# The tokens' low part in two products of 128 columns, once in each up stage

## The chip, the cores and the metric

The kernel runs on one core of one Trainium2 chip. The metric is the device time of one execution in microseconds; every comparison is between executions on the same chip. The profile shows one execution, with every instruction of the engines: PE is TensorE's matmuls, PEld its weight loads, DVE VectorE, ACT ScalarE, POOL GpSimd, SP the engine that issues the DMAs.

## What is computed

Two layers of an encoder trunk on 256 tokens with a model width of 2048, all in float32:

```python
h = rms_norm(x, g_pre_mix)
proj = h @ w_in                                  # 2048 x 4624
att = window_attention(...); mem = mlstm_mixer(...)
x = x + rms_norm(concat(att, mem) @ w_out, g_post_mix)
h = rms_norm(x, g_pre_mlp)
u = square(relu(h @ w_up))                       # 2048 x 8192
x = x + rms_norm(u @ w_down, g_post_mlp)         # 8192 x 2048
```

The change touches only the product `h @ w_up`.

## The kernel before, in words

**Products in three parts.** Each float32 operand is held as a high part (rounded to the format that TensorE takes, fp32r) and a low part (the rest). A product of two operands is then three matmuls into one PSUM sum: high by high, high by low, low by high. The weights come from HBM in pieces of 1 MB. `load` (lines 168 to 194) issues one DMA per piece on SP's queue into `raw` (two buffers), lets ACT write the high part `whi` (line 191) and DVE the low part `wlo` (line 192); there are four buffers of each. A tile's weights are asked for one tile ahead (lines 263 and 264).

**The order of the stages.** A layer runs ten tiles of the input product ("in", the first stage), four of "out", and then four blocks b = 0 to 3 of the MLP. Block b has an "up" stage of four tiles n = 0 to 3, 512 of the 8192 columns each, and a "down" stage of four tiles that uses them at once. The stages of both layers follow each other in the program; a framework that simulates the timeline places the instructions on the engines' queues, and can move small pieces of work (transposes, the mixing work of the heads) in between the large products.

**Two ways to run a product.** `mm_tile` (lines 220 to 257, products at lines 203 to 205) holds the tokens in the array and moves 512 columns of weights per product ("in" tiles 3 and 9 are narrower: 272 and 256 columns). `mm_stationary` (lines 259 to 275) does the opposite: it holds 128 columns of weights in the array and moves the 256 tokens. All up tiles run so, except tile 0 of block 0 in each layer, which runs in `mm_tile` because its tokens become ready one after another. So the up stage of block 0 has three tiles of this form and those of blocks 1 to 3 have four.

**The loop that the change touches.** A tile in `mm_stationary` has two pairs; a pair has two groups i of 128 weight columns, each with its own `whi` and `wlo`; a group sums over 16 chunks k of the model width. Each chunk is three products of 256 columns, each with a weight load of its own: `whi` by the tokens' high part (line 272), `whi` by their low part (line 273), `wlo` by their high part (line 274). That makes 48 products a group, 192 a tile, 768 in the up stage of blocks 1 to 3 and 576 in that of block 0. After each pair ACT squares the result from PSUM (`up_evac`, lines 846 to 850) while TensorE goes on in the other PSUM buffer.

In block 0 the tile before, run in `mm_tile`, has its results turned by four transposes of 128 columns (`ptu`, line 843). They stand in TensorE's queue inside the first pair of tile 1, in front of the last product of its first group.

Of the kernel before, what the change touches and what calls it, by code (L numbers as in the profile page):

```python
# [17 lines left out]
P = 128  # L18
SEQ = 256
# [56 lines left out]
def stationary(key):  # L76


    _, st, b, n = key
    return st == "up" and (b, n) != (0, 0)  # L80
# [6 lines left out]
def encoder_kernel(ctx, tc, x, wall, rope, conv_w, gate_bias, ml_g, sink, gpre, gpost, out):  # L87
    nc = tc.nc
# [70 lines left out]
    for l in range(DEPTH):  # L159
        for st, b, n, w in STAGES:  # L160
            key = (l, st, b, n)
# [6 lines left out]
    def load(i, begin=None):  # L168


        if i >= len(order) or order[i] in pieces:
            return
        o, w = offs[order[i]]
        k, n = (KC, P) if stationary(order[i]) else (PK, w)
        got = []
        for q in range(NPC):
            raw = wraw.tile([P, k, n], F32, tag="raw", name="raw")
            a = o + q * P * k * n
            src = wall[a:a + P * k * n].rearrange("(p k n) -> p k n", p=P, k=k)
            if begin is not None:  # L180
                begin(q)

            o1 = 16 if stationary(order[i]) else 0
            hi, lo = (
                wsp.tile([P, 2048 + 64], F32R, tag=x, name=f"w{x}")[:, o1:o1 + k * n].rearrange(
                    "p (k n) -> p k n", k=k) for x in ("hi", "lo"))
            step = 1 if begin is not None and q < 2 else k
            for j in range(0, k, step):
                sl = slice(j, j + step)
                nc.sync.dma_start(raw[:, sl], src[:, sl])  # L190
                nc.scalar.activation(hi[:, sl], raw[:, sl], AF.Copy)  # L191
                nc.vector.tensor_tensor(out=lo[:, sl], in0=raw[:, sl], in1=hi[:, sl].bitcast(F32), op=ALU.subtract)  # L192
            got.append((hi, lo))
        pieces[order[i]] = got
# [61 lines left out]
                after(t, ps[t])  # L256
        return ps

    def mm_stationary(key, T, after):

        load(pos[key])
        load(pos[key] + 1)
        for pair in range(2):
            both = psmm.tile([P, 2, 512], F32, tag="mm", name="mms")
            ps = both[:, 0].rearrange("p (i t) -> p i t", i=2)
            for i in range(2):
                hi, lo = pieces[key][2 * pair + i]
                for k in range(KC):  # L270
                    Tk = T[k // 8][:, k % 8]
                    nc.tensor.matmul(ps[:, i], lhsT=hi[:, k], rhs=Tk[:, 0], start=(k == 0), stop=False)  # L272
                    nc.tensor.matmul(ps[:, i], lhsT=hi[:, k], rhs=Tk[:, 1], start=False, stop=False)  # L273
                    nc.tensor.matmul(ps[:, i], lhsT=lo[:, k], rhs=Tk[:, 0], start=False, stop=(k == KC - 1))  # L274
            after(pair, ps)

# [28 lines left out]
    def rsq_part(ss, name):  # L305
        part = small.tile([P, 1], F32, tag="part", name=f"part_{name}")
        nc.vector.tensor_reduce(out=part, in_=ss, op=ALU.add, axis=AX.X)
        nc.vector.tensor_scalar(out=part, in0=part, scalar1=1.0 / DM, scalar2=EPS, op0=ALU.mult, op1=ALU.add)
        return part

    def square_sum(src, dst):
        junk = f1k.tile([P, 512], BF16, tag="junk", name="junk", bufs=1)
        nc.scalar.activation(junk, src, AF.Square, accum_out=dst)
# [6 lines left out]
    def new_T(name):  # L320
        return [tpool.tile([P, 8, 2, SEQ], F32R, tag="T", name=f"{name}{i}") for i in range(2)]

    def split_T(ps, hi, lo, eng=None):
        nc.scalar.activation(hi, ps, AF.Copy)  # L324
        (eng or nc.vector).tensor_tensor(out=lo, in0=ps, in1=hi.bitcast(F32), op=ALU.subtract)  # L325
# [15 lines left out]
    def pre_scale(t, name):  # L341

        ss = small.tile([P, 4], F32, tag="ss", name=f"ss_{name}")
        for n in range(4):
            square_sum(xs[:, t, n * 512:(n + 1) * 512], ss[:, n:n + 1])
        return rsq_row(rsq_part(ss[:, :3], name), ss[:, 3:4], f"{name}{t}")
# [312 lines left out]
    def pre_at(t, k, tp, T, norm):  # L659

        return {(t, k + i): (lambda i=i: pre(tp, i, T, norm)) for i in range(4)}

    for l in range(DEPTH):
# [74 lines left out]
        def in_tile(j, stages=(), at=None):  # L738
            return mm_tile((l, "in", 0, j), hT, stages, at=at)


        ps = in_tile(0, *in_stage)
# [12 lines left out]
        for grp in range(2):  # L755
            ps = in_tile(1 + grp)
            urgent.append(side_q(ps, grp))
        ps = in_tile(3)
        urgent.append(side_gates(ps))
        ps = in_tile(4)  # L760
        urgent.append(qk_heads(ps, 0, [1, 2], s1, cw, qk))
        ps = in_tile(5)
# [3 lines left out]
        ps = in_tile(6)  # L766
        urgent.append(side_v(ps, 0, 1, 2))
        ps = in_tile(7)
        urgent.append(side_v(ps, 0, 3, 1))
        urgent.append(side_gate(ps, 256, 0))  # L770
        ps = in_tile(8)
        urgent.append(side_gate(ps, 0, 1))
        urgent.append(side_gate(ps, 256, 2))
        ps = in_tile(9)
# [23 lines left out]
        h2T = []  # L798
# [32 lines left out]
        for b in range(4):  # L831
            uT = new_T("uT")
            for n in range(4):
                Tn = uT[n // 2]
                k0 = (n % 2) * 4

                def up_first(t, ps, Tn=Tn, k0=k0):
                    r = f2k.tile([P, 512], F32, tag="f2k", name="ur")
                    nc.scalar.activation(r, ps, AF.Relu)
                    nc.scalar.activation(r, r, AF.Square)  # L840
                    pt = psax.tile([P, 4, P], F32, tag="ax", name="ptu")
                    for i in range(4):
                        nc.tensor.transpose(pt[:, i], r[:, i * P:(i + 1) * P], ident)
                    split_T(pt, Tn[:, k0:k0 + 4, 0, t * P:(t + 1) * P], Tn[:, k0:k0 + 4, 1, t * P:(t + 1) * P])

                def up_evac(pair, ps, Tn=Tn, k0=k0):
                    z = f2k.tile([P, 2, SEQ], F32, tag="f2k", name="uz")
                    nc.scalar.activation(z, ps, AF.Relu)
                    nc.scalar.activation(z, z, AF.Square)
                    k = k0 + 2 * pair  # L850
                    split_T(z, Tn[:, k:k + 2, 0], Tn[:, k:k + 2, 1])

                key = (l, "up", b, n)
                if stationary(key):
                    mm_stationary(key, h2T, up_evac)
                else:
                    mm_tile(key, h2T, [(0, KC - PK)], up_first, pre_at(0, 6, 1, h2T, 2 * l + 1))
                    for t in range(NT):
                        s = pre_scale(t, "s2")
                        s2[t] = lay.tile([P, 1], F32, tag=f"s2q{t}", name="s2q")  # L860
                        nc.vector.tensor_tensor(out=s2[t], in0=s, in1=s, op=ALU.mult)
            for n in range(4):
                sl = slice(n * 512, (n + 1) * 512)

                def down_evac(t, ps, n=n, sl=sl, b=b):
                    if b == 0:
                        nc.scalar.activation(acc[:, t, sl], ps, AF.Copy, scale=s2[t])
                        return
                    nc.vector.scalar_tensor_tensor(  # L869
                        out=acc[:, t, sl], in0=ps, scalar=s2[t], in1=acc[:, t, sl], op0=ALU.mult, op1=ALU.add)  # L870
                    if b < 3:
                        return
                    square_sum(acc[:, t, sl], sd[t][:, n:n + 1])
                    if n == 2:
                        part[t] = rsq_part(sd[t][:, :3], f"rd{t}")
                    if n == 3:
                        r = rsq_row(part[t], sd[t][:, 3:4], f"rd{t}")
                    nc.vector.tensor_tensor(out=acc[:, t, sl], in0=acc[:, t, sl], in1=g[n], op=ALU.mult)
                    if n < 3:
                        return  # L880
                    if not last and not hT_next:
                        hT_next.extend(new_T("hT"))
                    for i in range(4):
                        residual(t, i, r)
                        if last:
                            si = slice(i * 512, (i + 1) * 512)
                            nc.sync.dma_start(out[t * P:(t + 1) * P, si], xs[:, t, si])

                key = (l, "down", b, n)
                if b < 3 or n < 3:  # L890
                    mm_tile(key, uT, after=down_evac)
                    if (b, n) == (3, 0):
                        g.append(gload(2 * l + 1, 3))
                else:
                    at = None if last else pre_at(1, 10, 0, hT_next, 2 * l + 2)
                    mm_tile(key, uT, [(PK, KC)], down_evac, at)
# [62 lines left out]
```

## Time and profile before

| | |
|---|---|
| median of 3 runs | 2146.42 us (2146.22 to 2150.07) |
| the profiled execution | 2146.89 us |
| its span, first to last instruction | 2145.1 us |
| PE busy | 2110.1 us, 98% of the span |
| DVE, ACT, POOL busy | 1134.4, 983.8, 60.4 us |
| products at lines 272, 273, 274 | 1920 each |
| from HBM | 384.39 MB read, 180 GB/s over the span |

Busy time of PE is the time in which at least one matmul is on record as running. Matmuls overlap in the records: a product of 256 columns is shown as some 280 ns long, but the next one starts long before it ends. What a stream of products costs is therefore read from the distance between their starts, not from their lengths. The layers' up and down stages lie at 383.7 to 1067 us and from 1449.6 us to the end; the stages of one kind have the same length in both layers but for block 0.

### The profile page before, as it was taken

To read this page: it belongs to the slowest core of one execution; us is meant where nothing else is said; L and a number is where in the kernel's file an instruction comes from. 1 tells how busy PE (TensorE), PEld (TensorE's weight loads), DVE (VectorE), ACT (ScalarE), POOL (GpSimd) and SP (SyncE) were. 2 spreads that over 40 slices of the span, in tenths; PEclk is the share of its full clock that TensorE was granted. 3 is DMA by queue.
4 is the path that set the end of the run, shared out by engine and by line. 5 is a ranking of instruction groups with operands and counts; after the bars stand their busy time and mean duration, and the time that the engine had idled before them with its cause. 6 is when DMAs were issued, how large, how long until landed. Compare 5 with 4: busy or idle time off the path is not lost.

```text
span 2145.1 us, 28978 instructions
## 1 busy us (share of the span) xinstructions
PE 2110.1 (98%) x12412; PEld 1868.9 (87%) x12412; DVE 1134.4 (53%) x1219; ACT 983.8 (46%) x1077; POOL 60.4 (3%) x68
## 2 busy tenths in 40 slices
PE   8999999999999999999999999999999999999998
PEld 6878887998998998898878788879889989989986
DVE  6656566544444444444567655575444444444444
ACT  5445544544443353354354555455445434434442
POOL 0000003000000000000020000030000000000000
PEclk9999999999999999999999999999999999999999
DMA  7435354555555555555444344546555555555553
GB/s 257 167 133 174 131 194 167 196 196 193 182 195 190 185 195 188 188 194 190 178 181 160 120 165 148 196 147 223 189 191 194 182 192 195 181 193 195 184 194 118
DMA packets 62209, 388.37 MB, mean 181 GB/s; under 512 B 9600, under 2 KB 10112, under 8 KB 17280
## 3 DMA queue, kind: packets, MB, share of 16 engines
q1 hardware_dynamic: 61936, 386.48, 51.2%
q8 instruction: 97, 1.59, 0.3%
q14 instruction: 32, 0.26, 0.0%
q10 hardware_dynamic: 144, 0.03, 0.0%
HBM read 384.39 MB, written 2.10 MB: 180 GB/s over the span
## 4 chain that ended last, share of the span: by engine, by line
PE 94%; DVE 2%; DMA 1%; ACT 1%; POOL 1%; issue 1%; SPq 0%; POOLq 0%; DVEq 0%; ACTq 0%
PE mm L205 19%; PE mm L203 19%; PE mm L204 19%; PE mms L274 11%; PE mms L272 10%; PE mms L273 10%; DMA raw<-wall 1%; PE pn L594 1%; PE sc L378 1%; PE po L417 1%; DVE xs L792 1%; POOL h2T L325 1%; ACT whi L191 0%; DVE wlo L192 0%; PE cp L577 0%
## 5 line engine op out<-in xcount | busy, mean ns | idle before, releaser
L192 DVE TENSOR_TENSOR wlo<-raw,whi 128x2048 fp32r<-128x2048 f32 (+3 forms) x374 | 828.7, 2217 | 884.5 <-ACT whi L191 884.1
L191 ACT ACTIVATE whi<-raw 128x2048 fp32r<-128x2048 f32 (+3 forms) x374 | 693.2, 1854 | 935.3 <-PE mm L205 511.0
L274 PE MATMUL mms<-h2T,wlo 128*128 128x256 f32 x1920 | 538.8, 281 | 0.0
L272 PE MATMUL mms<-h2T,whi 128*128 128x256 f32 x1920 | 538.6, 281 | 0.0
L273 PE MATMUL mms<-h2T,whi 128*128 128x256 f32 x1920 | 538.6, 281 | 0.0
L203 PE MATMUL mm<-whi,uT 128*128 128x512 f32 x1024 | 398.4, 389 | 0.0
L204 PE MATMUL mm<-wlo,uT 128*128 128x512 f32 x1024 | 398.4, 389 | 0.0
L205 PE MATMUL mm<-whi,uT 128*128 128x512 f32 x1024 | 398.0, 389 | 0.0
L273 PEld LDWEIGHTS mms<-h2T,whi 128*128 128x128 f32 x1920 | 367.1, 191 | 0.3
L274 PEld LDWEIGHTS mms<-h2T,wlo 128*128 128x128 f32 x1920 | 361.2, 188 | 0.0
L272 PEld LDWEIGHTS mms<-h2T,whi 128*128 128x128 f32 x1920 | 360.4, 188 | 0.3
L203 PE MATMUL mm<-whi,hT 128*128 128x512 f32 (+2 forms) x640 | 241.5, 378 | 8.8 <-ACT hT L324 6.5
L205 PE MATMUL mm<-whi,hT 128*128 128x512 f32 (+2 forms) x640 | 241.3, 378 | 1.2 <-POOL hT L325 1.1
L204 PE MATMUL mm<-wlo,hT 128*128 128x512 f32 (+2 forms) x640 | 239.8, 375 | 0.2 <-DVE wlo L192 0.2
L205 PEld LDWEIGHTS mm<-whi,uT 128*128 128x128 f32 x1024 | 192.3, 188 | 40.0
L203 PEld LDWEIGHTS mm<-whi,uT 128*128 128x128 f32 x1024 | 192.3, 188 | 39.6
L204 PEld LDWEIGHTS mm<-wlo,uT 128*128 128x128 f32 x1024 | 192.3, 188 | 39.5
L203 PEld LDWEIGHTS mm<-whi,hT 128*128 128x128 f32 x640 | 121.3, 190 | 29.2 <-ACT hT L324 7.6
L205 PEld LDWEIGHTS mm<-whi,hT 128*128 128x128 f32 x640 | 121.1, 189 | 22.5 <-POOL hT L325 2.0
L204 PEld LDWEIGHTS mm<-wlo,hT 128*128 128x128 f32 x640 | 121.2, 189 | 20.0 <-DVE wlo L192 0.5
L869 DVE SCALAR_TENSOR_TENSOR A_mlp<-mm,s2q,A_mlp 128x512 f32<-128x512 f32 x48 | 34.0, 747 | 37.2 <-PE mm L205 37.2
L203 PE MATMUL mm<-whi,memT 128*128 128x512 f32 x128 | 50.5, 395 | 0.0
(221 smaller groups left out, 1466.1 us busy)
## 6 DMA issues: line engine op xcount, KB each, us to landing
raw<-wall SPq DMA_DIRECT2D x350, 1024.0 KB, 4.8
raw<-wall SPq DMA_DIRECT2D x8, 544.0 KB, 3.5
g<-gpost SPq DMA_DIRECT2D x16, 256.0 KB, 4.6
raw<-wall SPq DMA_DIRECT2D x8, 512.0 KB, 3.3
xs<-x_in SPq DMA_DIRECT2D x8, 256.0 KB, 6.1
raw<-wall SPq DMA_DIRECT2D x8, 256.0 KB, 6.2
y_out<-xs SPq DMA_DIRECT2D x8, 256.0 KB, 2.8
cossin<-rope SPq DMA_DIRECT2D x1, 256.0 KB, 7.1
```

The lines of the kernel that those rows point to most:

```text
L191: nc.scalar.activation(hi[:, sl], raw[:, sl], AF.Copy)
L192: nc.vector.tensor_tensor(out=lo[:, sl], in0=raw[:, sl], in1=hi[:, sl].bitcast(F32), op=ALU.subtract)
L203: nc.tensor.matmul(dst, lhsT=xh, rhs=hi, start=(k == 0), stop=False)
L204: nc.tensor.matmul(dst, lhsT=xh, rhs=lo, start=False, stop=False)
L205: nc.tensor.matmul(dst, lhsT=xl, rhs=hi, start=False, stop=(k == KC - 1))
L272: nc.tensor.matmul(ps[:, i], lhsT=hi[:, k], rhs=Tk[:, 0], start=(k == 0), stop=False)
L273: nc.tensor.matmul(ps[:, i], lhsT=hi[:, k], rhs=Tk[:, 1], start=False, stop=False)
L274: nc.tensor.matmul(ps[:, i], lhsT=lo[:, k], rhs=Tk[:, 0], start=False, stop=(k == KC - 1))
L325: (eng or nc.vector).tensor_tensor(out=lo, in0=ps, in1=hi.bitcast(F32), op=ALU.subtract)
L378: nc.tensor.matmul(sc[:, j], lhsT=qT[:, q0 + j, t * P:(t + 1) * P], rhs=kT[:, g], start=(j == 0), stop=False)
L417: nc.tensor.matmul(po[:, j], lhsT=vA[:, kb, g * HD:(g + 1) * HD], rhs=pT[:, kb], start=(kb == 0), stop=(kb == 1))
L869: nc.vector.scalar_tensor_tensor(out=acc[:, t, sl], in0=ps, scalar=s2[t], in1=acc[:, t, sl], op0=ALU.mult, op1=ALU.add)
```

## The change

`mm_stationary` takes a new argument `apart`, the number of a pair. In that pair, in its first group (i = 0) and first chunk (k = 0), the product of `whi` and the tokens' low part is written as two matmuls of 128 columns, one for each half of the tokens, into the two halves of the same PSUM sum. Everywhere else `w` is 256 and the loop runs once, as before. `apart` is set for one tile in each up stage: pair 0 of tile 0 in blocks 1 to 3, and pair 1 of tile 1 in block 0. That is one product in each of the eight up stages.

```diff
-    def mm_stationary(key, T, after):
+    def mm_stationary(key, T, after, apart=None):
...
-                    nc.tensor.matmul(ps[:, i], lhsT=hi[:, k], rhs=Tk[:, 1], start=False, stop=False)
+                    w = P if (pair, i, k) == (apart, 0, 0) else SEQ
+                    for c in range(0, SEQ, w):
+                        nc.tensor.matmul(
+                            ps[:, i, c:c + w], lhsT=hi[:, k], rhs=Tk[:, 1, c:c + w], start=False, stop=False)
...
-                    mm_stationary(key, h2T, up_evac)
+
+                    apart = (0 if n == 0 else None) if b else (1 if n == 1 else None)
+                    mm_stationary(key, h2T, up_evac, apart)
```

## Rows read from the trace of the kernel before

**Rows 1.** Page, part 1: busy us (share of span) and instructions, TensorE.

```profile
PE 2110.1 (98%) x12412; PEld 1868.9 (87%) x12412; DVE 1134.4 (53%) x1219; ACT 983.8 (46%) x1077; POOL 60.4 (3%) x68
```

**Rows 2.** Page, part 4: the chain that ended last, by engine and line.

```profile
PE 94%; DVE 2%; DMA 1%; ACT 1%; POOL 1%; issue 1%; SPq 0%; POOLq 0%; DVEq 0%; ACTq 0%
PE mm L205 19%; PE mm L203 19%; PE mm L204 19%; PE mms L274 11%; PE mms L272 10%; PE mms L273 10%; DMA raw<-wall 1%; PE pn L594 1%; PE sc L378 1%; PE po L417 1%; DVE xs L792 1%; POOL h2T L325 1%; ACT whi L191 0%; DVE wlo L192 0%; PE cp L577 0%
```

**Rows 3.** Windows: length; PE, PEld, DVE, ACT, POOL busy; clock; DMA share; GB/s.

```profile
383.70:1067.00 683.30, 683.30 (x4401) 624.21 (x4401) 321.94 (x192) 299.85 (x239) 0.87 (x1) 1.00 0.54 192
...
383.70:451.90 68.20, 68.20 (x580) 68.16 (x580) 33.41 (x19) 35.30 (x31) 0.00 (x0) 1.00 0.57 202
539.10:629.50 90.40, 90.40 (x769) 90.40 (x768) 40.89 (x23) 44.05 (x39) 0.00 (x0) 1.00 0.53 187
...
1449.50:1515.40 65.90, 65.90 (x581) 65.90 (x580) 33.41 (x19) 35.27 (x31) 0.00 (x0) 1.00 0.60 208
```

**Rows 4.** Line 273 by window: count, min/median/max ns, first to last start.

```profile
L273 PE MATMUL mms<-h2T,whi x256: 280/281/281, 539.2 to 629.3; 128*128 128x256 f32 x128
...
L273 PE MATMUL mms<-h2T,whi x256: 280/281/281, 1957.7 to 2047.8; 128*128 128x256 f32 x128
...
L273 PE MATMUL mms<-h2T,whi x176: 281/281/281, 390.0 to 451.8; 128*128 128x256 f32 x176
...
L273 PE MATMUL mms<-h2T,whi x176: 276/276/277, 1455.7 to 1515.2; 128*128 128x256 f32 x176
```

**Rows 5.** Timeline of PE, layer 0, block 0: start us, length us.

```profile
389.16 0.28 PE L273 MATMUL mms<-h2T,whi 128*128 128x256 f32 x1
389.28 0.60 PE L843 MATMUL ptu<-ident,ur 128*128 128x128 f32 x4
389.63 0.36 PE L274 MATMUL mms<-h2T,wlo 128*128 128x256 f32 x1
389.83 0.28 PE L272 MATMUL mms<-h2T,whi 128*128 128x256 f32 x1
389.95 0.28 PE L273 MATMUL mms<-h2T,whi 128*128 128x256 f32 x1
```

**Rows 6.** Timeline of PE, layer 1, block 0, around the same transposes.

```profile
1454.79 0.28 PE L272 MATMUL mms<-h2T,whi 128*128 128x256 f32 x1
1454.91 0.28 PE L273 MATMUL mms<-h2T,whi 128*128 128x256 f32 x1
1455.03 0.60 PE L843 MATMUL ptu<-ident,ur 128*128 128x128 f32 x4
1455.38 0.37 PE L274 MATMUL mms<-h2T,wlo 128*128 128x256 f32 x1
1455.59 0.28 PE L272 MATMUL mms<-h2T,whi 128*128 128x256 f32 x1
1455.70 0.28 PE L273 MATMUL mms<-h2T,whi 128*128 128x256 f32 x1
1455.82 0.28 PE L274 MATMUL mms<-h2T,wlo 128*128 128x256 f32 x1
```

**Rows 7.** Timeline of PE at the start of the up stage, layer 0, block 1.

```profile
538.63 0.39 PE L204 MATMUL mm<-wlo,uT 128*128 128x512 f32 x1
538.86 0.39 PE L205 MATMUL mm<-whi,uT 128*128 128x512 f32 x1
539.09 0.28 PE L272 MATMUL mms<-h2T,whi 128*128 128x256 f32 x1
539.20 0.28 PE L273 MATMUL mms<-h2T,whi 128*128 128x256 f32 x1
539.32 0.28 PE L274 MATMUL mms<-h2T,wlo 128*128 128x256 f32 x1
```

**Rows 8.** Timeline of PE in "in" tile 9 of layer 1 (256 columns).

```profile
1321.17 0.28 PE L203 MATMUL mm<-whi,hT 128*128 128x256 f32 x1
...
1322.25 0.28 PE L203 MATMUL mm<-whi,hT 128*128 128x256 f32 x1
```

**Rows 9.** Waits: engine and line, waited for: us in total, times, longest.

```profile
ACT whi L191 <- PE mm L205: 511.0, 180, 5.3
ACT whi L191 <- PE mms L273: 320.8, 112, 3.7
ACT whi L191 <- DMA raw<-wall: 94.8, 45, 4.7
```

## The prediction

> **What bounds the kernel now.** I read the page's busy times first, then the chain of work that ended last, then the windows of the stages, then the starts of single products. The first two say TensorE: 98% busy [rows 1], 94% of the chain, with the three lines of `mm_stationary` at 31% of the span [rows 2]. The windows say that nothing else is late there: from 383.7 to 1067 us, all of layer 0's MLP, PE is busy 683.30 of 683.30 us at a clock of 1.00, the level of 2.4 GHz [rows 3]. The loaders wait for TensorE, not the other way round: ACT's high parts waited 320.8 us for the products of line 273 to free a buffer, and 94.8 us for the DMA [rows 9]. So in an up stage the time is the number of products times the distance between their starts, and nothing else.
>
> That distance is where the profile has something to show. In the six up stages of blocks 1 to 3, line 273 runs 256 times from 539.2 to 629.3 us (the last of the six: 1957.7 to 2047.8, the same 90.1 us) [rows 4]. 255 steps of three products make 765 distances: 90.1 / 765 = 117.8 ns. In block 0 of layer 0, after the transposes, 176 runs of the line take 390.0 to 451.8 us: 61.8 / 525 = 117.7 ns. In block 0 of layer 1, the same 176 runs on the same shapes take 1455.7 to 1515.2 us: 59.5 / 525 = 113.3 ns [rows 4]. The clock is 1.00 in both stages [rows 3]. **The same stream has two rhythms, 117.8 and 113.3 ns, 4.45 ns apart.** (The ends of the rows are rounded to 0.1 us, which leaves 0.2 ns of doubt in that.)
>
> Where does the second rhythm begin? Layer 1's stage also starts slow: 1454.79 to 1454.91 is 0.12 us. Then come the four transposes of 128 columns, and from then on the starts are 0.11, 0.12, 0.11 us apart [rows 6]. In layer 0 the same transposes stand at the same place and nothing changes [rows 5]. The two differ by one hundredth: the first full product behind the transposes is followed after 0.20 us (389.63 to 389.83) in layer 0 and after 0.21 us (1455.38 to 1455.59) in layer 1. The stream then holds its rhythm over eleven groups of 48 products, over borders of pairs and tiles, to the end of the stage [rows 4]. I read this as two stable ways in which weight loads and products can follow each other, with a short product as something that can push the stream from one into the other. The six stages that have no such push all run slow.
>
> **The change part by part.**
>
> *Removed and added.* Eight products of 256 columns become sixteen of 128, each with its own weight load (there is one per product: 12412 and 12412 [rows 1]). No DMA, no wait on another engine and no work of ACT or DVE is added, and none is moved past a queue. So first the price: eight extra pairs of load and product, on the engine that is the bound, with no cover. The trace has no product of 128 columns in this format. Lower end: time goes by columns (512 columns 0.23 us apart, 256 columns 0.12 [rows 7]), so two halves cost what the whole did: nothing. Upper end: the weight load sets the pace, and a half costs a whole distance, 0.118 us. The nearest row is the transposes, 128 columns too: four of them and the product behind take 389.28 to 389.83 = 0.55 us [rows 5], less one distance of 0.118 leaves 0.43, or 0.108 each. I take 0.11 us: 8 x 0.11 = 0.9 us more.
>
> *The rhythm.* In blocks 1 to 3 the halved product is the second of the stage, so 766 of 768 products follow it. If it pushes the stream into the fast rhythm, a stage saves 766 x 4.45 ns = 3.41 us, six stages 20.45 us. In block 0 it stands at the start of tile 1's second pair, behind the transposes; 96 + 384 = 480 products from there on, 478 behind it. Layer 0: 478 x 4.45 ns = 2.13 us saved. Layer 1 is already fast: nothing to gain, and 2.13 us to lose if the push throws it out.
>
> *Does it push?* Two halves put the array in the state that the transposes put it in: a short product is done before the next weights are in, so the next full product stands and waits for its load, where in the slow stream it follows with hardly a gap. Of two such events in the trace one changed the rhythm. The change from 512 columns to 256 at a stage's start, where the loads are long done, never did (all stages start at 0.12 us, [rows 7] for one). Since the instructions around the half are the same in the six stages and the six ran alike to 0.1 us, I expect them to fall alike. That makes it a little better than even, and the likeliest single case.
>
> *What is late next.* The faster stream needs its weights 4% sooner. Layer 1's block 0 has shown that they come: 208 GB/s and a DMA share of 0.60, against 187 GB/s and 0.53 in a slow stage, with ACT and DVE at half of the stage (35.27 and 33.41 of 65.9 us) and PE without a gap [rows 3]. The down stages behind run at their own distance and simply start earlier.
>
> *Sum.* -20.45 - 2.13 + 0.9 = -21.7 us. The profiled execution took 2146.89 us (span 2145.1 and 1.8 around it): 2125.2. It lay 0.5 us above the median of the runs, so against that median 2146.42 - 21.7 = 2124.7.
>
> [...] The starts in one format, of one shape and at one clock lie 113.3 or 117.8 ns apart [rows 4]. [...]
>
> **The rivals.**
>
> *No push.* The halves pass, and the stream falls back to 117.8 ns at once, as in layer 0 behind the transposes [rows 5]. For it: one event of two, and every stage start. Price: the 0.9 us alone, 2147.3; if layer 1's block 0 is thrown out of the fast rhythm too, 2149.4.
>
> *The rhythm is not history.* The distance is set by the columns and by something of layer 1's block 0 alone (buffers, transfers in the background). Then nothing can be pushed: 2146.4 to 2147.3. Against it: the distance changes within that stage at the transposes [rows 6] and then holds while weights buffers turn over. [...]
>
> *A slower rhythm.* This ends above. The trace has a third distance for 256 columns: in "in" tile 9 of layer 1, nine distances from 1321.17 to 1322.25 make 120.0 ns [rows 8], and it has the tokens as the weights there. If the halves push the stream to this one, six stages lose 766 x 2.2 ns = 1.7 us each, 10.1 us; layer 0's block 0 478 x 2.2 = 1.1; layer 1's, from 113.3, 478 x 6.7 = 3.2; with the 0.9 that is +15.3: 2161.7. It decides at the third start behind the halves, which would be 0.12 and not 0.11. Against it: neither event in `mm_stationary` went there.
>
> *Only some stages.* The push depends on jitter, as it did between the two layers, and about half of the stages change: -10 us, 2136.
>
> **How the numbers follow.** Chances: fast rhythm in all seven slow stages (or six, or with layer 1's block 0 lost) 0.54; some stages 0.06; no push 0.22; not history 0.05; slower rhythm 0.13. The likeliest gives 2124.7. Its own range: half products free (-0.9), the rounding of the 4.45 ns (0.2 ns x 5074 products, 1.0 each way), and one block 0 not going along or lost (+2.1, or +4.2 for both): 2123 to 2129. The range that holds the time 8 times in 10 runs from 2123 to 2150: that takes in the forecast, the partial case and both cases without a gain, and leaves out the slower rhythm and the tails, together under 2 in 10. A measurement of this kernel tells about 0.2% (4.3 us) from no change. Faster by more than that: 0.54 + 0.06 = 0.60. Within it: 0.22 + 0.05 = 0.27. Slower: 0.13.
>
> **What would show it.** Right: line 273 of blocks 1 to 3 with a span of some 86.7 us (765 x 113.3) instead of 90.1, from the product behind the halves on; starts of 0.11 us; lengths of 276 ns as in layer 1's block 0, not 281. The price: two starts of line 273 some 0.11 us apart where there was one. Wrong: a median of 281 ns and 90.1 us in these stages, or a rhythm of 120 ns; or the fast rhythm lost at a border of pairs or tiles; or PE with gaps in the up stages because the weights no longer come in time.

## The result, and the profile after

The changed kernel takes 2123.72 us (median of 4 runs, 2122.64 to 2126.88) against 2146.32 us before: a ratio of 0.9893, 95% interval 0.9876 to 0.9911, that is 1.1% faster. The forecast was 2124.7. In a second comparison it took 0.9918 of before (0.9898 to 0.9938; run e8 below).

The page of the changed kernel, part 1 and two of the three lines of part 5 for the products (line 273 is now the first, 276 the one with the halves, 278 the third):

```profile
PE 2083.9 (98%) x12420; PEld 1843.6 (87%) x12420; DVE 1135.6 (54%) x1219; ACT 984.5 (46%) x1077; POOL 60.5 (3%) x68
...
L278 PE MATMUL mms<-h2T,wlo 128*128 128x256 f32 x1920 | 530.8, 276 | 0.0
L276 PE MATMUL mms<-h2T,whi 128*128 128x256 f32 x1928 | 530.6, 276 | 0.0
```

The mean length of a product fell from 281 to 276 ns; before, 276 was the length in the one fast stage [rows 4]. There are eight loads and eight matmuls more (12420). PE is as busy as before, 98%; only the stages are shorter. The third product by stage (count, min/median/max ns, first to last start; layer 0 block 0, one of the six stages of blocks 1 to 3, layer 1 block 0):

```profile
L278 PE MATMUL mms<-h2T,wlo x192: 276/276/366, 383.1 to 448.8; 128*128 128x256 f32 x192
...
L278 PE MATMUL mms<-h2T,wlo x256: 276/276/335, 536.3 to 623.1; 128*128 128x256 f32 x128
...
L278 PE MATMUL mms<-h2T,wlo x192: 276/276/367, 1435.2 to 1500.9; 128*128 128x256 f32 x192
```

Each of the six takes 86.7 or 86.8 us where the same line took 90.1 us before. Nothing became late: the windows (length; PE, PEld, DVE, ACT, POOL busy; clock; DMA share; GB/s) of layer 0's MLP and of one stage show PE without a gap at the full clock, with the weights coming at 194 GB/s instead of 187 [rows 3]; and ACT still waits for TensorE more than for the DMA [rows 9].

```profile
380.90:1052.60 671.70, 671.70 (x4407) 612.48 (x4406) 321.87 (x190) 299.66 (x238) 0.00 (x0) 1.00 0.55 196
536.00:623.20 87.20, 87.20 (x770) 87.17 (x769) 40.89 (x23) 44.16 (x39) 0.00 (x0) 1.00 0.55 194
```
```profile
ACT whi L191 <- PE mms L276: 300.7, 112, 3.5
ACT whi L191 <- DMA raw<-wall: 82.6, 43, 4.6
```

The timeline of PE at the start of layer 0's block 1, which answers to [rows 7]:

```profile
536.02 0.28 PE L273 MATMUL mms<-h2T,whi 128*128 128x256 f32 x1
536.14 0.33 PE L276 MATMUL mms<-h2T,whi 128*128 128x128 f32 x2
536.31 0.34 PE L278 MATMUL mms<-h2T,wlo 128*128 128x256 f32 x1
536.48 0.28 PE L273 MATMUL mms<-h2T,whi 128*128 128x256 f32 x1
536.60 0.28 PE L276 MATMUL mms<-h2T,whi 128*128 128x256 f32 x1
536.72 0.28 PE L278 MATMUL mms<-h2T,wlo 128*128 128x256 f32 x1
536.84 0.28 PE L273 MATMUL mms<-h2T,whi 128*128 128x256 f32 x1
536.96 0.28 PE L276 MATMUL mms<-h2T,whi 128*128 128x256 f32 x1
537.07 0.28 PE L278 MATMUL mms<-h2T,wlo 128*128 128x256 f32 x1
537.18 0.28 PE L273 MATMUL mms<-h2T,whi 128*128 128x256 f32 x1
537.30 0.28 PE L276 MATMUL mms<-h2T,whi 128*128 128x256 f32 x1
```

The reader is to see three things. The price: the four products from 536.02 to 536.48 take 0.46 us where three took 0.35, so 0.11 us. (The halves themselves start only 0.06 us apart; the time goes to the product behind them, 0.17 us to the next start.) A stretch of four distances of 0.12 us behind it (536.48 to 536.96), in which the stream still looks slow. And from 536.96 on the rhythm of 0.11, 0.11, 0.12.

### The profile page after: what moved, and what is told of

It reads as the page before. It is cut to its first block, busy times and chain, and to the rows that moved or that the text cites. A ratio compares the mean times of both kernels' runs of the same rounds, so it can differ in the third digit from the quotient of the medians.

```text
span 2120.9 us, 28994 instructions
## 1 busy us (share of the span) xinstructions
PE 2083.9 (98%) x12420; PEld 1843.6 (87%) x12420; DVE 1135.6 (54%) x1219; ACT 984.5 (46%) x1077; POOL 60.5 (3%) x68
## 4 chain that ended last, share of the span: by engine, by line
PE 93%; DVE 2%; ACT 1%; DMA 1%; POOL 1%; issue 1%; SPq 0%; POOLq 0%; DVEq 0%; ACTq 0%
PE mm L205 19%; PE mm L203 19%; PE mm L204 19%; PE mms L278 10%; PE mms L276 10%; PE mms L273 10%; DMA raw<-wall 1%; PE pn L598 1%; PE sc L382 1%; DVE xs L796 1%; PE po L421 1%; DVE wlo L192 1%; POOL h2T L329 1%; ACT whi L191 0%; PE cp L581 0%
## 5 line engine op out<-in xcount | busy, mean ns | idle before, releaser
L278 PE MATMUL mms<-h2T,wlo 128*128 128x256 f32 x1920 | 530.8, 276 | 0.0
L276 PE MATMUL mms<-h2T,whi 128*128 128x256 f32 x1928 | 530.6, 276 | 0.0
L273 PE MATMUL mms<-h2T,whi 128*128 128x256 f32 x1920 | 530.2, 276 | 0.0
```

The lines of the kernel that those rows point to most:

```text
L276: nc.tensor.matmul(ps[:, i, c:c + w], lhsT=hi[:, k], rhs=Tk[:, 1, c:c + w], start=False, stop=False)
```

## The experiments

No run leaves out a part of the computation; an "extra" product goes into a PSUM bank that nothing reads. The tables of e1, e2, e6, e10 and e12 give the edits in words: layer, stage and block, and what is done at the first chunk of the stage where nothing else is said. The stages of blocks 1 to 3 start slow whatever the up stage ahead of them did: before the change, layer 1's block 1 is slow behind the fast block 0 of [rows 4].

```profile
L274 PE MATMUL mms<-h2T,wlo x256: 281/281/281, 1602.7 to 1692.8; 128*128 128x256 f32 x128
```

So one run can try six pushes, one in each up stage of blocks 1 to 3. What is read is the span of the third product in a stage, first to last start: 90.1 us is slow, 86.7 to 86.9 fast; the median length of a product tells the same (281 or 276 ns).

**e1: which product, and which parts?** In place of the one split of the change:

```diff
+    (0, 'up', 2, ...): low part as (192, 64)      (0, 'up', 3, ...): low part as (64, 192)
+    (1, 'up', 1, ...): third product halved       (1, 'up', 2, ...): first product of chunk 1 halved
+    (1, 'up', 3, ...): extra product of 256 columns behind the second
```

> One look at six up stages, each pushed in another way near its first products; block 0 of both layers and block 1 of layer 0 have no halves at all. A stage of blocks 1 to 3 lasts 90.34 us in the slow rhythm (117.8 ns) and 87.07 us in the fast one (113.3 ns). Layer 0: block 1 nothing, block 2 the low part as 192 + 64 columns, block 3 as 64 + 192. Layer 1: block 1 the third product (low weights) as 128 + 128, block 2 the first product of the second chunk as 128 + 128, block 3 an extra whole product of 256 columns into a spare PSUM bank, whose result is not used. Theory A (a product that is over before the next weights are in pushes the stream): five fast stages of 87.1 us, only the untouched block 1 and the whole extra product stay at 90.3 and 90.5. Theory B (any extra weight load pushes it): the whole extra product makes a fast stage too, 87.2. Theory C (it takes one certain delay, which 128 + 128 of the low part happens to give): 192 + 64 and 64 + 192 stay at 90.4, and so may the halved first and third product. All theories: block 1 of layer 0 at 90.3, since the down stages in between set the stream back.

Line 285, third product, layer 0 blocks 1 to 3 and layer 1 blocks 2 and 3:

```profile
L285 PE MATMUL mms<-h2T,wlo x256: 281/281/281, 540.2 to 630.3; 128*128 128x256 f32 x128
...
L285 PE MATMUL mms<-h2T,wlo x256: 276/276/365, 717.8 to 804.6; 128*128 128x256 f32 x128
...
L285 PE MATMUL mms<-h2T,wlo x256: 276/276/307, 892.1 to 978.8; 128*128 128x256 f32 x128
...
L285 PE MATMUL mms<-h2T,wlo x256: 276/276/281, 1769.8 to 1856.6; 128*128 128x256 f32 x128
...
L285 PE MATMUL mms<-h2T,wlo x256: 281/281/283, 1944.2 to 2034.3; 128*128 128x256 f32 x128
```

Every split pushes, whichever product it is and wherever it is cut; layer 1's block 1 took 86.8 us too. The stage without a push and the one with a whole extra product stay at 90.1. So it is not the tokens' low part, and not one more weight load as such: theory B falls, and theory C with it. (Four stages are fast, as theory A has it; the "five" in the expectation does not fit its own list.) The stage left alone stands behind a slow block 0 and so says nothing on whether a rhythm lives through a down stage; that it does not is shown by the line above, and again in e11.

**e2: where in the stage, and is it enough that one product is short?**

```diff
+    (0, 'up', 1, ...): extra 128      (0, 'up', 2, ...): halves at chunk 8
+    (0, 'up', 3, tile 2, ...): halves   (1, 'up', 1, ...): quarters of 64
+    (1, 'up', 2, ...): extra 32       (1, 'up', 3, ...): three products of chunk 1 halved
```

> One look at six up stages again, none in block 0. Layer 0: block 1 an extra product of 128 columns into a spare PSUM bank (its result is not used), block 2 the halves at chunk 8 of the first group, block 3 the halves at the start of tile 2. Layer 1: block 1 the low part in four quarters of 64, block 2 an extra product of 32 columns into the spare bank, block 3 all three products of the second chunk halved. Theory A: all six become fast from the push on: about 87.1 us, 87.2 (26 slow products before), 88.8 (384 slow products before), 87.3, 87.1 and 87.4. Theory C (one certain delay is wanted): the stages with the same 128 + 128 of the low part (layer 0, blocks 2 and 3) fast, the quarters, the 32 columns and the six halves by chance, 90.4 to 90.8 where they miss. Theory D (only the start of a stage can be pushed): layer 0's blocks 2 and 3 stay at 90.4.

Line 286, third product: layer 0 blocks 1 and 3, layer 1 block 1:

```profile
L286 PE MATMUL mms<-h2T,wlo x256: 281/281/332, 538.0 to 628.2; 128*128 128x256 f32 x128
...
L286 PE MATMUL mms<-h2T,wlo x256: 276/281/335, 889.9 to 978.5; 128*128 128x256 f32 x128
...
L286 PE MATMUL mms<-h2T,wlo x256: 276/276/367, 1597.1 to 1683.9; 128*128 128x256 f32 x128
```

The splits push anywhere: at chunk 8 (86.9 us), in the middle of the stage (88.6, half slow and half fast), in quarters (86.8) and three in a row (87.1). Theory D falls. But a single short product does not: the extra 128 leaves 90.2 us, and the extra 32 too. The timeline shows that it does all that the forecast asked of a push. The product behind the short one (538.01) starts 0.06 us after it and is shown as 0.33 us long, with 0.17 us to the next start, as behind the halves of the change:

```profile
537.95 0.22 PE L292 MATMUL mms<-h2T,whi 128*128 128x128 f32 x1
538.01 0.33 PE L286 MATMUL mms<-h2T,wlo 128*128 128x256 f32 x1
538.18 0.40 PE L286 MATMUL mms<-h2T,whi 128*128 128x256 f32 x2
```

Theory A, mine, falls with that.

The price of an extra product does not go by its columns. The products with `whi` in a slow stage, first to last start, with 32 columns more (line 286, this run) and with 256 more (line 285, e1):

```profile
L286 PE MATMUL mms<-h2T,whi x512: 280/281/281, 1771.0 to 1861.4; 128*128 128x256 f32 x171
```
```profile
L285 PE MATMUL mms<-h2T,whi x512: 280/281/281, 1943.8 to 2034.2; 128*128 128x256 f32 x171
```

Both take 90.4 us. In the starts of the traces the whole stage takes 90.45 us with either, 90.33 without: an extra product costs one distance, as in the prediction's upper end.

**e6: two short products in a row, or a split?**

```diff
+    (0, 'up', 1): extra 128 + 128     (0, 'up', 2): the two halves one chunk apart
+    (0, 'up', 3): halves; extra 128 at tile 2      (1, 'up', 1): halves; extra 32 at tile 2
+    (1, 'up', 2): extra 32 + 32       (1, 'up', 3): extra 128 + 128 + 128
```

> One look at six up stages, none pushed in block 0. So far every split of a product into parts made the fast rhythm, and every single extra product (256, 128 or 32 columns, into a spare bank) left the slow one. Theory F: it takes two short products in direct succession; one alone sets the slow rhythm, even in a fast stream. Theory G: it takes a split, that is one more load for the same number of columns, or writes to the same bank; extra columns into a spare bank do nothing. Layer 0: block 1 two extra products of 128 into the spare bank (F fast, 87.3 us; G slow, 90.6); block 2 the two halves of the low part put apart, the second one after the third product of the next chunk (F slow, 90.4; G fast, 87.1); block 3 the halves at the start and one extra product of 128 at the start of tile 2 (F slow again from there, 88.8; G fast to the end, 87.2). Layer 1: block 1 the halves at the start and one extra product of 32 at tile 2 (F 88.8, G 87.2); block 2 two extra products of 32 (F fast, 87.2; G slow, 90.5); block 3 three extra products of 128 (F fast, 87.4; G slow, 90.7).

Line 289, third product: layer 0 blocks 1 to 3, layer 1 block 2:

```profile
L289 PE MATMUL mms<-h2T,wlo x256: 276/276/333, 538.8 to 625.5; 128*128 128x256 f32 x128
...
L289 PE MATMUL mms<-h2T,wlo x256: 276/276/331, 712.9 to 799.8; 128*128 128x256 f32 x128
...
L289 PE MATMUL mms<-h2T,wlo x256: 276/281/335, 887.3 to 975.8; 128*128 128x256 f32 x128
...
L289 PE MATMUL mms<-h2T,wlo x256: 281/281/363, 1770.0 to 1860.2; 128*128 128x256 f32 x128
```

Both theories miss. Two extra 128s push although nothing is split, against G; the halves put apart push although each stands alone, and two extra 32s do not, against F. What stays is the third stage, and layer 1's block 1 with the same 88.6 us: **a single short product in the middle throws a fast stream back into the slow rhythm** (128 columns in the one, 32 in the other). A push works both ways.

**e10 and e12: is there an order in what pushes?** Extra products behind the second product, as in e6, of other sizes; then six of them again, each in another stage.

```diff
+    e10: (0, 'up', 1..3): extra 64 + 64; 96 + 96; 192     (1, 'up', 1..3): extra 96; 192 + 192; 128 + 32
+    e12: (0, 'up', 1..3): extra 96; 32 + 32; 192 + 192    (1, 'up', 1..3): extra 128; 64 + 64; 192
```

> One look, offset 16, nothing in block 0; extra products into the spare bank behind the second product of blocks 1 to 3. So far 256, 128, 32 and 32 + 32 columns left the slow rhythm and 128 + 128 and 128 + 128 + 128 ended it. Layer 0: 64 + 64, 96 + 96, 192. Layer 1: 96, 192 + 192, 128 + 32. Theory F2 (two products in succession that are not too short): 96 + 96 and 192 + 192 fast (87.2 and 87.3 us), 64 + 64 unclear, singles slow (90.4 to 90.5), 128 + 32 slow. Theory H (only where the delay lands in the period counts, not how many products make it): fast and slow come in no order of number or size, and a single product of 96 or 192 columns can push.

> The extra products once more, each in another stage than before, to see whether the outcome goes with the pattern or with the stage and chance. Layer 0: block 1 one of 96 columns (fast before), block 2 two of 32 (slow before), block 3 two of 192 (slow before). Layer 1: block 1 one of 128 (slow before), block 2 two of 64 (fast before), block 3 one of 192 (fast before). If it goes with the pattern: fast, slow, slow, slow, fast, fast (87.1, 90.6, 90.6, 90.4, 87.2, 87.1 us). If with chance, about half of the six differ from that.

e10, line 286, third product: layer 0 block 3 (192) and layer 1 blocks 1 (96) and 2 (192 + 192):

```profile
L286 PE MATMUL mms<-h2T,wlo x256: 276/276/302, 885.6 to 972.3; 128*128 128x256 f32 x128
...
L286 PE MATMUL mms<-h2T,wlo x255: 276/276/347, 1588.9 to 1675.3; 128*128 128x256 f32 x128
...
L286 PE MATMUL mms<-h2T,wlo x256: 281/281/304, 1763.3 to 1853.4; 128*128 128x256 f32 x128
```

Together, extra products behind the second one, by what the stage did after:

| | fast | slow |
|---|---|---|
| one | 96, 192 | 32, 128, 256 |
| two | 64 + 64, 96 + 96, 128 + 128 | 32 + 32, 128 + 32, 192 + 192 |
| three | 128 + 128 + 128 | |

Neither number nor size orders this, as theory H had it, and F2 falls (192 + 192). Yet it is no chance: in e12 all six came out as before, in other stages (86.8, 90.2, 90.2, 90.2, 86.7, 86.7 us). Two of them, one of 96 and one of 128 columns:

```profile
L286 PE MATMUL mms<-h2T,wlo x256: 275/277/348, 542.2 to 629.0; 128*128 128x256 f32 x128
...
L286 PE MATMUL mms<-h2T,wlo x256: 280/282/332, 1601.3 to 1691.5; 128*128 128x256 f32 x128
```

A single 96 looks in the timeline of e10 much like the single 128 of e2 (0.05 and 0.18 us against 0.06 and 0.17); one pushes and the other does not:

```profile
1588.82 0.21 PE L292 MATMUL mms<-h2T,whi 128*128 128x96 f32 x1
1588.87 0.35 PE L286 MATMUL mms<-h2T,wlo 128*128 128x256 f32 x1
1589.05 0.40 PE L286 MATMUL mms<-h2T,whi 128*128 128x256 f32 x2
```

The traces hold starts to the nanosecond, and there the two distances are 44 and 185 ns against 60 and 168. Their sum is the same to 1 ns, and so it is with 192 columns (89 and 139) and with 32 (28 and 200): 228 or 229 ns each time, and two of the four push. So theory H's outcome came, but not its reason: the delay that an extra product leaves does not tell the ones that push from the others. What does is in no row.

**e3, e9 and e5: does it matter where the weights lie?** The offset of the weights in their buffers, by block (16 elements before):

```diff
-            o1 = 16 if stationary(order[i]) else 0
+            o1 = shift(order[i])     # e3, e5: 0, 8, 32; 48, 64, 4     e9: 12, 20, 24; 28, 40, 56
```

> No halves anywhere; the weights of an up stage lie at another offset in their buffers (in 4-byte elements; 16 before): layer 0 blocks 1 to 3 at 0, 8 and 32, layer 1 blocks 1 to 3 at 48, 64 and 4; block 0 stays at 16. Theory A alone (the rhythm is a matter of which came first, load or product): all six stages keep 117.8 ns, 90.3 us. Theory E (weight loads and moved tokens meet in the same part of SBUF, and the rhythm is how they fall into step): the stages differ with the offset, some at 113.3 ns without any push (86.9 us), some at 120 ns (92.0 us), and offsets that are equal in their low bits behave alike.

> No halves; six more offsets of the weights in their buffers: layer 0 blocks 1 to 3 at 12, 20 and 24 elements, layer 1 blocks 1 to 3 at 28, 40 and 56 (so far 0, 32 and 64 gave 120.0 ns, 4 and 8 about 118.5, 16 and 48 117.8). If the slow rhythm is a matter of where weights and tokens meet within 32 elements (128 bytes), 40 repeats 8 (90.8 us), 56 equals 24, and the values run between 90.3 and 92.0 us with the least about 16 and 48. If some offset keeps weights and tokens apart altogether, that stage runs at 113.3 ns without a push, 86.9 us, and would be a version without extra products.

> The halves at the start of blocks 1 to 3 (none in block 0), and the weights at the offsets of the run before with six offsets: layer 0 blocks 1 to 3 at 0, 8 and 32 elements, layer 1 blocks 1 to 3 at 48, 64 and 4. Without halves these stages took 92.03, 90.76, 92.04, 90.34, 92.03 and 90.76 us. If the fast rhythm is one in which weight loads and moved tokens no longer meet, whatever the address, all six come to 87.07 us. If it exists only at offsets of 16 modulo 32, layer 1's block 1 (48) comes to 87.07 and the others stay where they were plus 0.1 for the extra product: 92.2, 90.9, 92.2, 92.2, 90.9.

Third product, line 289, in e3 (layer 0 block 1 at offset 0; layer 1 block 1 at 48) and in e9 (layer 1 block 3 at 56), then line 295 in e5 with the halves (layer 0 block 3 at 32; layer 1 block 1 at 48):

```profile
L289 PE MATMUL mms<-h2T,wlo x256: 283/283/283, 539.4 to 631.2; 128*128 128x256 f32 x128
...
L289 PE MATMUL mms<-h2T,wlo x256: 277/280/280, 1608.7 to 1698.8; 128*128 128x256 f32 x128
```
```profile
L289 PE MATMUL mms<-h2T,wlo x256: 277/278/281, 1960.9 to 2050.2; 128*128 128x256 f32 x128
```
```profile
L295 PE MATMUL mms<-h2T,wlo x256: 279/281/333, 895.6 to 986.4; 128*128 128x256 f32 x128
...
L295 PE MATMUL mms<-h2T,wlo x256: 277/280/334, 1602.8 to 1693.0; 128*128 128x256 f32 x128
```

The rhythm without a push depends on the offset. In us for the stage: 91.8 at 0, 32, 64, 28 and 40 (120.0 ns); 90.7 at 20; 90.5 at 4, 8 and 12; 90.1 at 16 and 48; 89.8 at 24; 89.3 at 56 (116.7 ns). No offset gives 113.3 by itself, and the repeat after 32 elements that I expected is not there (8 and 40 differ, 24 and 56 differ). These figures are means over a stage. To the nanosecond the distance is even at 0 and 64 (120 each time), but at others it runs through a pattern over and over: 118, 120, 122 at 32; 119, 114, 122, 119, 126 at 28; about 120, 113, 116, 118 at 56. The same mean can hide different patterns. With the halves of the change, none of the six offsets of e5 becomes fast: 48 stays at 90.2, 0 and 64 at 91.8 and 91.9, 8 and 4 at 90.6 and 90.5; 32 moves from 91.8 to 90.8, so there the halves do end the rhythm, but for another one (118.7 ns). **Of the seven offsets tried with the halves, only the 16 that the kernel has gives the 3.3 us a stage.** Whether another push would do it at another offset was not tried. The Trainium skill, "TensorE: Matmul & The Clock Gate", section "Step-by-step: what each phase is for", says that loading the next weights takes no read bandwidth from the running product; no run here shows whether that is so. The place of the weights alone moves the mean distance of the same products between 116.7 and 120.0 ns, and the length of the loads does not go with it (192 ns at offset 0, 187 or 188 at 40 in the median, 120.0 ns apart in both), but whether a load holds up a product there or something else does is not told apart.

**e11: another order of the three products.**

```diff
+                    run = [(k, j) for k in range(KC) for j in (0, 2, 1)]                      # swap
+                    run = [(k, j) for k in range(KC) for j in ((0, 1, 2), (2, 1, 0))[k % 2]]  # snake
+                    run = [(k, j) for j in range(3) for k in range(KC)]                       # part
```

> The same products in another order, offset 16. Before: per chunk high by high, high by low, low by high (weights by tokens). Layer 0 block 1 and 2: the second and third product of each chunk swapped, block 2 with the product behind the first one halved; layer 0 block 3 and layer 1 block 1: every second chunk in reverse order, layer 1 block 1 with halves; layer 1 blocks 2 and 3: all 16 high by high, then all high by low, then all low by high, block 3 with halves. If the rhythm comes from which loads and tokens run beside each other, these orders differ from 117.8 ns: where a stream of equal products meets nothing new, 113.3 or 120.0 throughout (86.9 or 92.0 us), and the halves may do nothing. If it is only the history of the stream, the unpushed ones take 90.3 us and the halved ones 87.1.

All three orders run at a median length of 281 ns without halves and 276 with them, six stages of six. Line 292, layer 0 block 3 (snake, no halves, behind a fast block 2) and layer 1 block 3 (part, halves; the products with `wlo` come last in a group there, so their span is shorter):

```profile
L292 PE MATMUL mms<-h2T,wlo x256: 281/281/281, 891.6 to 981.4; 128*128 128x256 f32 x128
...
L292 PE MATMUL mms<-h2T,wlo x256: 276/276/277, 1953.9 to 2037.2; 128*128 128x256 f32 x128
```

So the rhythms do not come from the change between high and low parts; the stream has both at this offset in each of the four orders tried. History decides, as the second half of the expectation had it.

**e4, e8 and e7: the transposes of block 0, and a better version.** e4 puts the halves of block 0 ahead of the transposes; e8 is the changed kernel again; e7 has halves ahead of and behind them, and in the narrow "in" tiles too.

```diff
+    (0, 'up', 0, 1, 0, 0, 0): {1: (128, 128)},     # e4, e7: block 0, tile 1, pair 0; layer 1 alike
...
+    (0, 'up', 0, 1, 1, 0, 0): {1: (128, 128)},     # e7: block 0, tile 1, pair 1 too; layer 1 alike
...
+narrow = {(0, 0), (0, 4), (0, 8), (0, 12)}         # e7: first half of the tokens, chunks 0, 4, 8, 12
```

> The changed kernel with one thing moved: in block 0 the halves stand in the first pair of tile 1, ahead of the transposes, not behind them. Blocks 1 to 3 as in the changed kernel: six stages of 87.07 us. Theory A: block 0 is fast from its second product on; if the transposes leave a fast stream alone, 576 products at 113.3 and the transposes' 0.4 us make 65.7 us in both layers, 0.4 to 0.5 less than behind a slow first group. If the transposes can throw a fast stream out, block 0 ends slow, some 67.9 us. Whole time: 2123 us, 22 to 24 less than before.

> The changed kernel once more, on this chip and beside the others: 0.989 of before, 2123 us. All theories: six stages of 87.07 us. Block 0 of layer 0 shows whether the halves behind the transposes mend a stage that these left slow: 66.0 us where they do or the transposes pushed it themselves, 68.3 where it stays slow.

> A version that would be faster than both: halves in block 0 at the start of tile 1 and again behind the transposes, so that both of its rhythms are set, and in the two narrow in tiles (272 and 256 columns, 125 and 120.0 ns a product before) the low part of weights of four chunks in two halves each. Blocks 1 to 3 as in the changed kernel: six stages of 87.07 us. Block 0: 65.8 to 66.0 us in both layers, against 68.16 where the transposes leave it slow. The narrow tiles: if halves push there too, tile 9 goes from 120.0 to 113.3 ns and tile 3 from 125 to 120; at most 0.6 + 0.5 us a layer, less 8 extra products of 0.1 us each, so little or nothing is left. Whole time: 2122 us, 0.989 of before, not to be told from the changed kernel.

Third product, e4 (line 288), block 0 of layer 0 and of layer 1; then e8 (line 278), block 0 of layer 0:

```profile
L288 PE MATMUL mms<-h2T,wlo x192: 276/281/335, 383.7 to 451.5; 128*128 128x256 f32 x192
...
L288 PE MATMUL mms<-h2T,wlo x192: 276/276/335, 1439.8 to 1505.2; 128*128 128x256 f32 x192
```
```profile
L278 PE MATMUL mms<-h2T,wlo x192: 276/276/363, 385.4 to 451.4; 128*128 128x256 f32 x192
```

In e4 the transposes throw layer 0's stream out of the fast rhythm that the halves had given it (67.8 us, median 281), and leave layer 1's alone. Over the fourteen profiles of this study the stream is fast behind the transposes of layer 1 every time, and behind those of layer 0 six times. In e8 they left layer 0 slow and the halves behind them mended it: 66.0 us, against 67.9 before, where the stream stayed as [rows 5] leave it. In the first profile of the changed kernel the transposes had done it themselves. There line 278, from the first product behind the transposes to the halves, is at 276 ns:

```profile
388.78 0.37 PE L278 MATMUL mms<-h2T,wlo 128*128 128x256 f32 x1
388.98 0.28 PE L273 MATMUL mms<-h2T,whi 128*128 128x256 f32 x1
```
```profile
L278 PE MATMUL mms<-h2T,wlo x15: 276/276/279, 389.2 to 394.0; 128*128 128x256 f32 x15
```

The runs differ there by a few nanoseconds. In twelve profiles layer 0's stream was slow when it met the transposes. The last distance ahead of them was 123 or 124 ns in the six that stayed slow, and 120 in five of the six that became fast (123 in the sixth, e11). That goes with the outcome; it does not show why.

Times: e4 0.9904 of before (0.9882 to 0.9925), e8 0.9918 (0.9898 to 0.9938), e7 0.9923 (0.9908 to 0.9938). e7's block 0 took 65.9 and 65.6 us, but its halves in tile 9 of layer 1 changed nothing there: it returned to 120 ns after each. It is no faster than the changed kernel.

## Why the prediction was right

- *The bound.* Right. The time is the number of products times their distance, and the gain is in the distance alone: six stages from 90.1 to 86.8 us, 20 us of the 22.6.
- *The price.* Forecast 0.11 us a split; measured 0.11 (0.46 for 0.35 us), plus a short stretch of slow distances behind it. An extra product costs the same with 32 columns as with 256 (e2).
- *The saving in a stage.* Forecast 3.41 less 0.11; measured 90.1 less 86.8, 3.3 us, alike in all six stages and in all four runs that had the change's splits there (the first, e4, e7, e8).
- *Block 0.* Forecast 2.1 us in layer 0 and nothing in layer 1; measured 67.9 to 65.7 (2.2) and 65.6 to 65.7. In the first run of the change layer 0's gain was not the halves' doing, since the transposes had pushed the stream already, by luck and not by the change; e8 shows that the halves do it when those have not.
- *That the rhythm is history.* Right, and the rival that held it for a matter of block 0 alone is refuted, by the push itself. But it is history at one place of the weights: which slow rhythm there is, and whether the halves end it, goes by the offset (e3, e5, e9). That the offset counts was in none of my cases.
- *What makes a push.* Wrong. I wrote that a short product puts the array in a state where the next one waits for its weights, and that this pushes. Single products of 32 and 128 columns do that and push nothing, or push the wrong way (e2, e6). Nor was the hundredth between 0.20 and 0.21 us behind the transposes the mark of a push: in the changed kernel layer 0's transposes pushed with 0.20 (388.78 to 388.98). That the halves landed well was luck in so far as this argument goes. Of twelve kinds of extra product six push and six do not, about the "little better than even" that it gave. Every split tried in a slow stream at offset 16 pushed (e1, e2, e6, e11), and why splits always do and extra products only half of the time is open.
- *The slower rhythm* that I feared did not come, though it is real: the same stream runs at 120.0 ns when its weights lie at offset 0 (e3). The sign that was to tell it, a third start behind the halves after 0.12 us and not 0.11, came all the same: the starts behind the halves are 0.12 us apart up to 536.96, and fast only from there.
- *The rest.* The stages explain 6 x 3.3 + 2.2 - 0.1 = 21.9 of the 24.2 us between the two profiled spans (2145.1 and 2120.9). The remainder lies outside the up stages and varies between runs: from the last up product of layer 0 to the first third product of layer 1's block 0 it is 465.2 us before (984.5 to 1449.7), 463.6 after (971.6 to 1435.2), and 465.3 and 467.2 in e2 and e3, which share that stretch.

What stays open is the mechanism: what holds the stream at one distance or the other. The outcomes fit a stream that can lock in more than one phase; no row shows the phase.

## What to carry to other kernels

Where a stream of equal matmuls is the bound, compare the distance between starts from stage to stage: two distances for the same shape at the same clock, with the operands at the same offsets, mean that the stream has more than one rhythm, and the cheapest experiment is one split product near the start of the stage. Do not reason out which disturbance helps; try a handful, one per stage of a single run, and look for the distance to hold to the end of the stage. Keep the operands' offsets fixed while doing so, since the push found at one place in the buffer did not bring the fast rhythm at six others.

## What was not expected of the hardware

- A stream of 256-column products with one weight load each has one of several mean distances at the same clock of 1.00: 113.3 and 117.8 ns at one offset of the weights, 116.7 to 120.0 ns at others, there in part as a pattern of unequal distances that repeats (e9). It keeps it over 700 products and over borders of tiles.
- The same disturbance gives the same rhythm each time it meets the same stream (six of six repeated in e12; the transposes of layer 0's block 0, whose timing varies by a few nanoseconds, do not), while columns 32, 96, 128, 192 and 256 of one extra product give slow, fast, slow, fast, slow.
- The place of the stationary operand in its buffer, in steps of 16 bytes, changes the mean distance without a push from 116.7 ns (offset 56) to 120.0 (offset 0).
- An extra product of 32 columns costs the slow stream as much as one of 256: 0.12 us (e2, e1).
